# Stick-breaking attention block: a filler clock that counts all matmuls, a head norm issued in four steps, an output projection in two passes, and masks added two blocks at a time

## Chip, core and metric

The kernel runs on one core of a Trainium2 chip. The time is the device time of one execution in microseconds (us); the figure compared is the median of the timed runs. TensorE (PE) multiplies, PEld is its weight load, ScalarE (ACT) does activations, VectorE (DVE) elementwise work, GpSimd (POOL) little here, and SyncE (SP) issues the weight transfers.

## Reference, cut to what matters

The program computes two transformer blocks on 512 tokens of width 1024: block one (feed-forward, two attention branches, feed-forward), block two (feed-forward, stick-breaking attention, feed-forward). The change lies in the stick-breaking attention, 16 heads of 64 wide:

```
qkv = (xn @ w_qkv).reshape(b, s, 3, 16, 64)
q = rms_norm(qkv[:, :, 0], q_gain);  k = rms_norm(qkv[:, :, 1], k_gain);  v = qkv[:, :, 2]
z = q @ k.T / sqrt(64)                      # per head, blocks of 128 queries
mask = s_idx < t_idx                        # strictly causal
log_1m = where(mask, log_sigmoid(-z), 0)
rev_excl = reverse exclusive cumsum of log_1m over the keys
w = where(mask, exp(log_sigmoid(z) + rev_excl), 0)
o = (w @ v) over all heads;   x = x + o @ w_o
```

## The kernel before, in words

All activations are kept transposed, 128 features by 512 tokens to a tile. Every large product is done in three matmuls of 32-bit "round" type (`mm3`, lines 182 to 184): a weight chunk of 128x128 and an activation tile are each split into a high and a low part, and high x high, high x low and low x high are added in PSUM. One `mm3` on one 128-row slice is a **unit**; a tile of width 1024 needs eight. Weight chunks come in by SP in the order of the list `plan`; `split_ahead` makes the high part on ACT (line 159, "cast") and the low part on DVE (line 160), four chunks ahead of their use. PE, ACT and SP execute in the order in which the code writes them; DVE and POOL instructions are placed by the framework.

The stick-breaking stage weaves two strands. `stick()` is the attention of eight head pairs n = 0..7. `sb_dense()` is the filler: 128 units of Q and K projections (`qk_tile`), 64 units of V (`sv_tile`, six matmuls of 256 columns each), and then the first units of the output projection. `stick()` hands over at each `yield s`, whereupon `F.pull(s)` writes s filler units. `F.t` is a clock that goes on by one with each unit pulled; `F.at(d, fn)` has `fn` written when the clock has gone d further.

A head pair is written thus. `front`: 14 score matmuls (line 853), two for block 2 of the upper head (858), and eight matmuls of 128 columns that add the causal mask (862); the scores fill five PSUM banks A1, A0, Z2, B1, B0 of the eight. Then six steps t = 0..5: absolute value from PSUM (`absolute`, line 868, DVE), Exp and Ln (872, 873, ACT), `soft` (877, DVE), and the high/low split of the result (177 ACT, 178 DVE). Then `middle(…, 0)`, 20 records of cumulative-sum matmuls (887, 892, 893) on the lower head's banks, `middle(…, 1)` on the upper head's, Exp of the five banks (`weights`, 896, ACT), and `back(n-1)`, the product with V of the pair before (905), whose result is split and put in `os_` three ticks later. `front(n)` waits, in the writing, until K[n] is there; `back` until the clock is past `state["bank_free"]`.

The head norm of a Q or K tile: `first` (one tick after its eighth unit) scales the tile out of PSUM on DVE (778) and squares it on ACT (780); `second`, seven ticks later (`NORM_LAG`), sums over each head by a matmul (786, called hn below), and at once writes Ln and Exp (211, 212, ACT) and four DVE instructions (214, 215, 216, 789); nine ticks later (`SCALE_LAG`) the tile counts as there. A Q tile's K tile follows right behind it in the filler.

The output projection: `EARLY = ((0, 1), (2,))` runs tiles 0 and 1, then 2, over os_[0..6] into PSUM banks that stay taken; behind the stage tile 3 is done whole, then the last unit of 0, 1 and 2, then tiles 4 to 7. After each tile DVE adds it to x (972), and ACT and DVE prepare the next feed-forward (227 or 230, 231, 249, 250).

Of the kernel before, what the change touches and what calls it, by code (L numbers as in the profile page):

```python
# [16 lines left out]
P = 128  # L17
S = 512
D = 1024
KD = 8  # L20
# [15 lines left out]
class Flow:  # L36
# [19 lines left out]
    def pull(self, n):  # L56

        for _ in range(n):
            got = 0 if self.dense is None else next(self.dense, 0)
            self.t += 1  # L60
            self.fire()
            if got == 0:
                self.dense = None
            if got != 1:
                return False
        return True

    def settle(self):
        while self.due:
# [5 lines left out]
def block_kernel(ctx: ExitStack, tc: tile.TileContext, a, out):  # L75
# [56 lines left out]
    for kind, n in SB_ORDER:  # L132
        if kind == "v":
            sv_chunks(n)
        else:
            plan.append((a["sb_qk"][n], 1024))
            plan.append((a["sb_qk"][8 + n], 1024))
    for m in range(KD):
        plan.append((a["sb_o"][m], 1024))
    for n in range(2 * NF):  # L140
        plan.append((a["f4_in"][n], 1024))
# [627 lines left out]
    def qk_tile(n, which, g):  # L769
        ps = bank()  # L770
        yield from proj(ps, a["sb_qk"][n], 1024, zs)
        if "r2" not in state:
            state["r2"] = nx.rstd()
            F.at(7, lambda: column_of(state["r2"], rcol2))

        def first():
            t = sl()
            dve.tensor_tensor(t, ps, state["r2"], op=OP.mult)
            sq = sl()
            act.activation(sq, t, AF.Square)  # L780
            F.at(NORM_LAG, lambda: second(t, sq))

        def second(t, sq):
            pm = bank()
            state["bank_free"] = F.t + 6
            pe.matmul(pm, halves, sq, start=True, stop=True)  # L786
            rs = sl()
            rsqrt(rs, pm, 1.0 / 64)
            dve.scalar_tensor_tensor(t, t, g, rs, op0=OP.mult, op1=OP.mult)
            if which is K:  # L790
                pool.tensor_copy(kz[n % 3][HALF[1], :], t[HALF[1], 2 * P:3 * P])
            F.at(SCALE_LAG, lambda: which.__setitem__(n % 8, t))
        F.at(1, first)

    def sb_dense():
        for kind, n in SB_ORDER:
            if kind == "v":
                yield from sv_tile(n)
            else:
                yield from qk_tile(n, Q, qg)  # L800
                yield from qk_tile(8 + n, K, gains[:, 57:58])

        for ms in EARLY:
            for m in ms:
                early.append((bank(), weight(a["sb_o"][m], 1024)))
            split_ahead(SPLIT_AHEAD + 1 - len(early))
            for k in range(7):
                while os_[k] is None:
                    yield 2
                for m in ms:  # L810
                    ps, (wh, wl) = early[m]
                    c = slice(k * P, (k + 1) * P)
                    mm3(ps, wh[:, c], wl[:, c], *os_[k], k == 0, False)
                    yield 1

    early = []
    os_ = [None] * KD
    HALF = (slice(0, 64), slice(64, 128))
    kz = [consts.tile([P, P], F32, name=f"kz{i}") for i in range(3)]
# [7 lines left out]
    ident_r = consts.tile([P, P], F32R, name="ident_r")  # L827
    dve.tensor_copy(ident_r, ident)

    hidden_r = consts.tile([P, P], F32R, name="hidden_r")  # L830
    dve.scalar_tensor_tensor(hidden_r, later, NEG, ident_n, op0=OP.mult, op1=OP.add)
    nlater = consts.tile([P, P], F32, name="nlater")
    dve.scalar_tensor_tensor(nlater, later, -1.0, ident, op0=OP.mult, op1=OP.subtract)
    nones = consts.tile([P, P], F32, name="nones")
# [7 lines left out]
    def stick():  # L842

        def front(n):

            q, k = Q[n], K[n]
            z = [bank() for _ in range(5)]
            started = set()  # L850
            for g, sb in ((0, 1), (1, 1), (0, 3), (1, 3), (0, 0), (1, 0), (0, 2)):
                b, c = AT[g][sb]
                pe.matmul(z[b][:, c:c + S - sb * P], k[HALF[g], sb * P:(sb + 1) * P], q[HALF[g], sb * P:],  # L853
                          start=b not in started, stop=True, skip_group_check=True)
                started.add(b)

            b, c = AT[1][2]
            pe.matmul(z[b][:, c:c + 2 * P], kz[(8 + n) % 3], q[:, 2 * P:], start=False, stop=True, skip_group_check=True)
            for sb in (1, 3, 0, 2):
                for g in range(2):  # L860
                    b, c = AT[g][sb]
                    pe.matmul(z[b][:, c:c + P], ident_r, hidden_r, start=False, stop=True, skip_group_check=True)
            return z

        def absolute(z, b):

            t = sl()
            dve.tensor_scalar(t.bitcast(I32), z[b].bitcast(I32), 0x7FFFFFFF, None, op0=OP.bitwise_and)
            return t

        def log_part(t):
            act.activation(t, t, AF.Exp, scale=-1.0)
            act.activation(t, t, AF.Ln, bias=1.0)

        def soft(t, z):

            dve.scalar_tensor_tensor(t, z, 0.0, t, op0=OP.max, op1=OP.add)

        def middle(z, sp, hl, g):
            for j in ((3, 1, 0, 2), (3, 1, 2, 0))[g]:  # L880
                bj, cj = AT[g][j]
                w = S - j * P
                for sb in range(j, -1, -1):
                    b, c = AT[g][sb]
                    dst = z[b][:, c + (j - sb) * P:c + (j - sb) * P + w]
                    if w == P:
                        pe.matmul(dst, nlater if j == sb else nones, sp[bj][:, cj:cj + w], start=False, stop=True,
                                  skip_group_check=True)
                        continue
                    hi, lo = hl[bj]  # L890
                    m = nlater_r if j == sb else nones_r
                    pe.matmul(dst, m, hi[:, cj:cj + w], start=False, stop=True, skip_group_check=True)  # L892
                    pe.matmul(dst, m, lo[:, cj:cj + w], start=False, stop=True, skip_group_check=True)  # L893

        def weights(z, t, b):
            act.activation(t[b], z[b], AF.Exp)

        def back(n, t):

            po = bank()  # L900
            for sb in range(4):
                for g in range(2):
                    b, c = AT[g][sb]
                    cv = (sb % 2) * 256 + (n % 2) * P + g * 64
                    pe.matmul(po[HALF[g], sb * P:], v[sb // 2][n // 2][:, cv:cv + 64], t[b][:, c:c + S - sb * P],  # L905
                              start=sb == 0, stop=sb == 3)
            pair = split(po)
            F.at(3, lambda: os_.__setitem__(n, pair))

        last = None  # L910
        for n in range(KD):
            while n not in K and F.pull(1):
                pass
            while n not in K:
                F.t += 1
                F.fire()
            z = front(n)
            sp, hl = {}, {}
            order = (A1, A0, Z2, B1, B0)
            for t in range(6):  # L920

                for b in order[:2] if t == 0 else order[t + 1:t + 2]:
                    sp[b] = absolute(z, b)
                if t < 5:
                    log_part(sp[order[t]])
                if 1 <= t:
                    soft(sp[order[t - 1]], z[order[t - 1]])
                if 2 <= t < 5:
                    hl[order[t - 2]] = split(sp[order[t - 2]])
                yield 3 if t < 4 else 1  # L930
            middle(z, sp, hl, 0)
            hl[B1] = split(sp[B1])
            yield 1
            hl[B0] = split(sp[B0])
            yield 3
            weights(z, sp, A1)
            weights(z, sp, A0)
            middle(z, sp, hl, 1)
            for b in (B1, Z2, B0):
                weights(z, sp, b)  # L940
            yield 1
            if n:
                while F.t < state["bank_free"] and F.pull(1):
                    pass
                while v[1][(n - 1) // 2] is None and F.pull(1):
                    pass
                back(n - 1, last)
            yield 2
            last = sp
        yield 7  # L950
        back(KD - 1, last)
# [7 lines left out]

    norm = Norm()  # L960
    xs = [None] * KD
    ne = len(early)
    for m in [ne] + list(range(ne)) + list(range(ne + 1, KD)):
        if m < ne:
            ps, (wh, wl) = early[m]
            c = slice(7 * P, 8 * P)
            mm3(ps, wh[:, c], wl[:, c], *os_[7], False, True)
            split_ahead()
        else:
            ps = bank()  # L970
            run(proj(ps, a["sb_o"][m], 1024, os_))
        dve.tensor_tensor(x[m], ps, x[m], op=OP.add)
        norm.add(x[m])
        xs[m] = scaled_split(x[m], gain(G_F2, m))
# [16 lines left out]
ROPE_LAG = 10  # L991
STACK_LAG = 5
BACK = 3
NORM_LAG = 7
SCALE_LAG = 9
VALUE_LAG = 4
EARLY = ((0, 1), (2,))
MIX_HEAD = [T_KI, 0, 1, 2, 3]
MIX_BODY = [T_QA, T_KA, T_QA + 1, T_KA + 1, T_QA + 2, T_KA + 2, T_QA + 3, T_KA + 3, T_QB, T_QB + 1, T_QB + 2,
            T_QB + 3, T_KB] + list(range(T_GA, T_GA + 16))  # L1000
# [88 lines left out]
```

## Time and profile before

| | us |
|---|---|
| median of 3 runs (lowest, highest) | 2160.03 (2158.42, 2160.56) |
| the profiled execution | 2160.37 |
| its span in the trace | 2158.6 |
| the stick-breaking stage in it (end of feed-forward three to the last `back`) | about 1481 to 1758 |

The span runs from the first to the last instruction; what the execution takes beyond it is 1.8 us. A view by windows gives, for a stretch that one chooses, the time in which each engine had an instruction running. PE instructions overlap at their ends, so the time from one start to the next, not the duration, is what a matmul costs in a row of matmuls.

### The profile page before, as it was taken

What the parts mean: (1) busy time and instruction counts of PE and PEld (TensorE: products, weight loads), DVE (VectorE), ACT (ScalarE), POOL (GpSimd) and SP (SyncE); (2) the same over time, 40 slices, a digit from 0 to 9 for tenths busy, and PEclk for the clock granted to TensorE, in tenths of its full rate; (3) what the DMA queues carried; (4) which work ended last, traced back from release to release, by engine and by line L of the source; (5) the groups of instructions that cost most, each with busy time, mean ns of one, the idle gap of its engine ahead of it and who ended that gap; (6) DMA issues with size and microseconds to landing.
All of it is one profiled execution on the core that took longest, in us unless ns stands there. A gap on an engine that the chain in (4) does not pass through costs nothing.

```text
span 2158.6 us, 24839 instructions
## 1 busy us (share of the span) xinstructions
PE 2124.3 (98%) x10038; PEld 1748.6 (81%) x10038; DVE 1092.6 (51%) x1608; ACT 827.8 (38%) x1287; POOL 11.9 (1%) x42
## 2 busy tenths in 40 slices
PE   8999999999999999999999999999999999999999
PEld 6888888887888888888888888887777778888887
DVE  6444334699944744443445444345675556444322
ACT  5222222376766432222333222224564544222211
POOL 0000000000000000000000000000000000000000
PEclk9999999999999999999999999999999999999999
DMA  4333333322212333333333333332111113333331
GB/s 163 107 97 98 90 100 110 107 79 74 80 49 74 113 103 95 96 97 93 97 94 98 97 98 95 98 100 79 49 40 49 40 57 110 98 98 98 91 120 54
DMA packets 57266, 193.42 MB, mean 90 GB/s; under 512 B 6784, under 2 KB 6784, under 8 KB 57152
## 3 DMA queue, kind: packets, MB, share of 16 engines
q1 hardware_dynamic: 55296, 188.28, 28.1%
q0 software_dynamic: 640, 2.10, 0.3%
q8 instruction: 78, 1.28, 0.2%
q10 hardware_dynamic: 1216, 1.47, 0.2%
q14 instruction: 36, 0.29, 0.0%
HBM read 189.07 MB, written 2.10 MB: 89 GB/s over the span
## 4 chain that ended last, share of the span: by engine, by line
PE 89%; DVE 7%; ACT 3%; issue 1%; DMA 0%; ACTq 0%; DVEq 0%
PE ps L182 27%; PE ps L183 27%; PE ps L184 27%; DVE wl L160 1%; PE ps L905 1%; PE ps L853 1%; PE ps L542 1%; DVE sl L497 1%; PE ps L599 1%; PE ps L893 1%; PE ps L530 1%; DVE m L495 1%; PE ps L786 0%; PE ps L892 0%; PE ps L754 0%
## 5 line engine op out<-in xcount | busy, mean ns | idle before, releaser
L182 PE MATMUL ps<-sl,wh 128*128 128x512 f32 x2704 | 1069.7, 396 | 6.6 <-ACT sl L249 6.6
L183 PE MATMUL ps<-sl,wh 128*128 128x512 f32 x2704 | 1056.7, 391 | 1.7 <-DVE sl L250 1.6
L184 PE MATMUL ps<-sl,wl 128*128 128x512 f32 x2704 | 1056.1, 391 | 0.0
L182 PEld LDWEIGHTS ps<-sl,wh 128*128 128x128 f32 x2704 | 510.1, 189 | 116.2 <-issue 6.6
L183 PEld LDWEIGHTS ps<-sl,wh 128*128 128x128 f32 x2704 | 510.2, 189 | 107.9 <-issue 3.4
L184 PEld LDWEIGHTS ps<-sl,wl 128*128 128x128 f32 x2704 | 509.8, 189 | 107.7
L159 ACT ACTIVATE wh<-wraw 128x1024 fp32r<-128x1024 f32 (+3 forms) x368 | 372.8, 1015 | 534.0 <-issue 242.4
L160 DVE TENSOR_TENSOR wl<-wraw,wh 128x1024 fp32r<-128x1024 f32 (+3 forms) x368 | 431.4, 1174 | 283.2 <-ACT wh L159 282.6
L177 ACT ACTIVATE sl<-sl 128x512 fp32r<-128x512 f32 x145 | 90.0, 627 | 388.9 <-DVE sl L279 384.0
L279 DVE TENSOR_TENSOR sl<-ps,sl 128x512 f32<-128x512 f32 x88 | 60.8, 691 | 267.1 <-PE ps L184 260.7
L178 DVE TENSOR_TENSOR sl<-sl 128x512 fp32r<-128x512 f32 x145 | 99.0, 689 | 67.9 <-ACT sl L177 67.4
L277 DVE TENSOR_TENSOR sl<-ps,sl 128x512 f32<-128x512 f32 x88 | 60.8, 690 | 138.8 <-PE ps L184 138.7
L230 ACT ACTIVATE sl<-x 128x512 f32<-128x512 f32 x42 | 25.8, 627 | 114.0 <-DVE x L299 97.5
L298 DVE SCALAR_TENSOR_TENSOR sl<-ps,sl 128x512 f32<-128x512 f32 x32 | 22.1, 691 | 79.9 <-PE ps L184 79.9
L278 ACT ACTIVATE sl<-sl 128x512 f32<-128x512 f32 x88 | 54.1, 615 | 12.2 <-DVE sl L277 12.1
L516 ACT ACTIVATE sl<-sl,mx 128x128 f32<-128x128 f32 (+3 forms) x64 | 35.7, 558 | 41.4 <-DVE mx L515 41.2
L523 ACT ACTIVATE sl<-sl,sm 128x128 f32<-128x128 f32 (+3 forms) x64 | 35.9, 560 | 25.3 <-DVE sm L522 14.8
L599 PE MATMUL ps<-sl 128*128 128x256 f32 (+2 forms) x176 | 43.2, 327 | 0.8 <-DVE mx L515 0.8
L231 DVE TENSOR_TENSOR sl<-sl 128x512 f32<-128x512 f32 x49 | 33.3, 690 | 18.7 <-ACT sl L230 18.2
L754 PE MATMUL ps<-wh,sl 128*128 128x256 f32 x128 | 40.4, 316 | 0.0
L599 PEld LDWEIGHTS ps<-sl 128*128 128x128 f32 x176 | 33.1, 189 | 8.6 <-DVE mx L515 1.3
L214 DVE SCALAR_TENSOR_TENSOR sl<-sl 128x512 f32<-128x512 f32 x23 | 15.9, 692 | 46.9 <-ACT sl L212 46.8
(136 smaller groups left out, 1291.0 us busy)
## 6 DMA issues: line engine op xcount, KB each, us to landing
wraw<-in_f_in_dram SPq DMA_DIRECT2D x176, 512.0 KB
wraw<-in_f_out_dram SPq DMA_DIRECT2D x64, 512.0 KB
wraw<-in_mix_t_dram SPq DMA_DIRECT2D x34, 512.0 KB
wraw<-in_f_out_dram SPq DMA_DIRECT2D x32, 384.0 KB
wraw<-in_sb_qk_dram SPq DMA_DIRECT2D x16, 512.0 KB
wraw<-in_br_dram SPq DMA_DIRECT2D x16, 256.0 KB
wraw<-in_w_out_dram SPq DMA_DIRECT2D x8, 512.0 KB
wraw<-in_sb_v_dram SPq DMA_DIRECT2D x8, 512.0 KB
```

What stands on the lines that cost most here:

```text
L159: act.activation(wh[:, :n], raw[:, :n], AF.Copy)
L160: dve.tensor_tensor(wl[:, :n], raw[:, :n], wh[:, :n].bitcast(F32), op=OP.subtract)
L177: act.activation(h, x, AF.Copy)
L178: dve.tensor_tensor(l, x, h.bitcast(F32), op=OP.subtract)
L182: pe.matmul(ps, wh, xh, start=start, stop=False)
L183: pe.matmul(ps, wh, xl, start=False, stop=False)
L184: pe.matmul(ps, wl, xh, start=False, stop=stop)
L277: dve.tensor_tensor(g, pg, rs, op=OP.mult)
L278: act.activation(g, g, AF.Silu)
L279: dve.tensor_tensor(g, pu, g, op=OP.mult)
L599: pe.matmul(ps[:, :n], q[:, i * P:(i + 1) * P], part[:, :n], start=x_ == 0, stop=x_ == 1)
L754: pe.matmul(dst, hh, wh[:, cl], start=kk == 0 and b == 0, stop=False)
```

## The change

- `F.tick(n)` moves the clock on by n without pulling filler. It is called with 4 behind `front`, 4 behind the first `middle`, 2 behind the second and 3 behind `back`.
- The head norm is written in four steps: scaling on DVE; two ticks later the square on ACT; `NORM_LAG` (now 4) later the matmul; two ticks later Ln, Exp and the DVE instructions; `SCALE_LAG` (now 8) later the tile is there. `bank_free` is set to eight ticks behind the matmul instead of six.
- The masks of the blocks that lie in one bank are added by one matmul: two of 128 columns (A0, B0), and three of 256 columns (A1, Z2, B1) whose output is two separate runs of 128 columns in the bank. `hidden_r` is doubled for it by one more DVE instruction, once.
- The absolute value of A1 and B1 moves from DVE to ACT (`AF.Abs`).
- At step t = 4 two filler units are pulled where it was one, and at t = 5 likewise.
- The output projection runs in two passes. Tiles 0 to 4 take their first 5, 5, 6, 6, 6 slices while the stage runs, and DVE adds them to x; behind the stage tile 5 is done whole, then the remaining 3, 3, 2, 2, 2 slices of tiles 0 to 4, then tiles 6 and 7. The weight chunks of tiles 0 to 4 are loaded and split in two parts each.

```diff
+    def tick(self, n):
+        for _ in range(n):
+            self.t += 1
+            self.fire()
...
-    for m in range(KD):
+    for m, w in enumerate(SBO_K):
+        plan.append((a["sb_o"][m][:, :w * P], w * P))
+    plan.append((a["sb_o"][len(SBO_K)], 1024))
+    for m, w in enumerate(SBO_K):
+        plan.append((a["sb_o"][m][:, w * P:], 1024 - w * P))
+    for m in range(len(SBO_K) + 1, KD):
         plan.append((a["sb_o"][m], 1024))
...
         def first():
             t = sl()
             dve.tensor_tensor(t, ps, state["r2"], op=OP.mult)
+            F.at(2, lambda: second(t))
+
+        def second(t):
             sq = sl()
             act.activation(sq, t, AF.Square)
-            F.at(NORM_LAG, lambda: second(t, sq))
-
-        def second(t, sq):
+            F.at(NORM_LAG, lambda: third(t, sq))
+
+        def third(t, sq):
             pm = bank()
-            state["bank_free"] = F.t + 6
+            state["bank_free"] = F.t + 8
             pe.matmul(pm, halves, sq, start=True, stop=True)
+            F.at(2, lambda: fourth(t, pm))
+
+        def fourth(t, pm):
             rs = sl()
             rsqrt(rs, pm, 1.0 / 64)
...
-        for ms in EARLY:
-            for m in ms:
-                early.append((bank(), weight(a["sb_o"][m], 1024)))
-            split_ahead(SPLIT_AHEAD + 1 - len(early))
-            for k in range(7):
+        for m, w in enumerate(SBO_K):
+            ps = bank()
+            wh, wl = weight(a["sb_o"][m][:, :w * P], w * P)
+            for k in range(w):
                 while os_[k] is None:
                     yield 2
-                for m in ms:
-                    ps, (wh, wl) = early[m]
-                    c = slice(k * P, (k + 1) * P)
-                    mm3(ps, wh[:, c], wl[:, c], *os_[k], k == 0, False)
-                    yield 1
+                c = slice(k * P, (k + 1) * P)
+                mm3(ps, wh[:, c], wl[:, c], *os_[k], k == 0, k == w - 1)
+                if k == w - 1:
+                    split_ahead()
+                yield 1
+            F.at(1, lambda m=m, ps=ps: dve.tensor_tensor(x[m], ps, x[m], op=OP.add))
...
-            for sb in (1, 3, 0, 2):
-                for g in range(2):
-                    b, c = AT[g][sb]
-                    pe.matmul(z[b][:, c:c + P], ident_r, hidden_r, start=False, stop=True, skip_group_check=True)
+            for b in (A1, A0, Z2, B1, B0):
+                blocks = z[b].rearrange("p (a c) -> p a c", a=4)
+                n_ = 1 if b in (A0, B0) else 2
+                blocks = blocks[:, 0:1] if n_ == 1 else blocks[:, 0:3:2] if b == Z2 else blocks[:, 0:4:3]
+                pe.matmul(blocks, ident_r, hidden_r[:, :n_ * P].rearrange("p (a c) -> p a c", a=n_), start=False,
+                          stop=True, skip_group_check=True)
...
         def absolute(z, b):
             t = sl()
+            if b in (A1, B1):
+                act.activation(t, z[b], AF.Abs)
+                return t
...
             z = front(n)
+            F.tick(4)
...
-                yield 3 if t < 4 else 1
+                yield 3 if t < 4 else 2
             middle(z, sp, hl, 0)
+            F.tick(4)
...
             middle(z, sp, hl, 1)
+            F.tick(2)
...
                 back(n - 1, last)
+                F.tick(3)
...
-    ne = len(early)
-    for m in [ne] + list(range(ne)) + list(range(ne + 1, KD)):
-        if m < ne:
-            ps, (wh, wl) = early[m]
-            c = slice(7 * P, 8 * P)
-            mm3(ps, wh[:, c], wl[:, c], *os_[7], False, True)
-            split_ahead()
-        else:
-            ps = bank()
-            run(proj(ps, a["sb_o"][m], 1024, os_))
+    ne = len(SBO_K)
+    for m in [ne] + list(range(KD)):
+        if m == ne and xs[m] is not None:
+            continue
+        ps = bank()
+        w = SBO_K[m] if m < ne else 0
+        src = a["sb_o"][m][:, w * P:] if w else a["sb_o"][m]
+        run(proj(ps, src, 1024 - w * P, os_[w:], 0, KD - w))
...
-NORM_LAG = 7
-SCALE_LAG = 9
+NORM_LAG = 4
+SCALE_LAG = 8
-EARLY = ((0, 1), (2,))
+SBO_K = (5, 5, 6, 6, 6)
```

## Rows read from the trace of the kernel before

**Rows 1.** The page: busy time of each engine, and the chain that ended last, by engine.

```profile
PE 2124.3 (98%) x10038; PEld 1748.6 (81%) x10038; DVE 1092.6 (51%) x1608; ACT 827.8 (38%) x1287; POOL 11.9 (1%) x42
PE 89%; DVE 7%; ACT 3%; issue 1%; DMA 0%; ACTq 0%; DVEq 0%
```

**Rows 2.** Windows: stretch and length, busy us (instructions) of PE, PEld, DVE, ACT, POOL, granted clock.

```profile
1736.00:1757.80 21.80, 21.80 (x132) 16.24 (x130) 13.04 (x20) 12.65 (x22) 0.00 (x0) 1.00 0.15 49
1757.80:1800.00 42.20, 42.20 (x188) 34.92 (x187) 24.90 (x33) 19.02 (x27) 0.00 (x0) 1.00 0.30 94
```

**Rows 3.** Waits of PE, 1481 to 1758: total us, times, longest.

```profile
PE ps L892 <- ACT sl L177: 9.9, 9, 2.5
PE ps L893 <- DVE sl L178: 6.0, 12, 0.8
```

**Rows 4.** Windows of PE alone: the eight `middle` with waits, first, longest, sum.

```profile
1516.48:1521.90 5.42, 3.82 (x22) 1.00 0.00 1
...
1712.47:1720.06 7.59, 4.31 (x23) 0.79 0.10 40
sum 45.92, PE 29.97; mean PE 3.75
```

**Rows 5.** Windows of PE alone: the filler behind four of them, low clock, first and sum.

```profile
1551.62:1556.60 4.98, 4.98 (x13) 0.52 0.34 96
...
sum 15.47, PE 15.47; mean PE 3.87
```

**Rows 6.** Windows of PE alone: 48 filler matmuls, mask, `middle`, 42 V matmuls, whole `front`.

```profile
1470.11:1480.99 10.88, 10.88 (x50) 1.00 0.23 89
1505.00:1506.03 1.03, 1.03 (x11) 1.00 0.33 131
1525.60:1528.37 2.77, 2.77 (x23) 1.00 0.12 49
...
1600.93:1606.01 5.08, 5.08 (x44) 1.00 0.00 0
...
1627.72:1631.45 3.73, 3.73 (x26) 1.00 0.02 4
```

**Rows 7.** Waits of ACT, 1481 to 1758.

```profile
ACT sl L780 <- DVE sl L778: 38.7, 13, 3.6
...
ACT sl L211 <- PE ps L786: 19.1, 12, 5.9
```

**Rows 8.** Timeline at 1502: start, us, engine, line, what, [idle before].

```profile
1502.42 0.63 ACT L212 ACTIVATE sl<-sl 128x512 f32<-128x512 f32 x1
1503.09 0.69 DVE L214 SCALAR_TENSOR_TENSOR sl<-sl 128x512 f32<-128x512 f32 x1 [0.70 <-ACT sl L212]
...
1505.15 0.68 DVE L778 TENSOR_TENSOR sl<-ps,sl 128x512 f32<-128x512 f32 x1
...
1505.87 0.64 ACT L780 ACTIVATE sl<-sl 128x512 f32<-128x512 f32 x1 [2.81 <-DVE sl L778]
```

**Rows 9.** Groups of instructions, 1481 to 1758: busy us, mean ns | idle before.

```profile
L873 ACT ACTIVATE sl<-sl 128x512 f32<-128x512 f32 x40 | 25.3, 632 | 1.3
L159 ACT ACTIVATE wh<-wraw 128x1024 fp32r<-128x1024 f32 x24 | 25.1, 1045 | 0.1
L177 ACT ACTIVATE sl<-ps 128x512 fp32r<-128x512 f32 x8 | 4.8, 597 | 18.4 <-PE ps L905 18.4
```

**Rows 10.** The chain that ended last: a head-norm matmul, its two records together.

```profile
1652.88 0.86 PE ps L786 x2
```

**Rows 11.** Groups of instructions on DVE, 1757.8 to 1800.

```profile
L160 DVE TENSOR_TENSOR wl<-wraw,wh 128x1024 fp32r<-128x1024 f32 x9 | 10.9, 1220 | 5.2 <-ACT wh L159 5.2
L972 DVE TENSOR_TENSOR x<-ps,x 128x512 f32<-128x512 f32 x8 | 5.4, 685 | 10.6 <-PE ps L184 10.5
```

**Rows 12.** Table loads in the whole trace, by groups: the line that loads for Silu.

```profile
L278 ACT ACT_TABLE_LOAD x4 | 5.1, 1283 | 0.1
```

More of the change, by code (lines that the diff above doesn't have):

```diff
@@ L801, in sb_dense @@
                 yield from qk_tile(8 + n, K, gains[:, 57:58])
-        for ms in EARLY:
-            for m in ms:
-                early.append((bank(), weight(a["sb_o"][m], 1024)))
-            split_ahead(SPLIT_AHEAD + 1 - len(early))
-            for k in range(7):
+        for m, w in enumerate(SBO_K):
+            ps = bank()
+            wh, wl = weight(a["sb_o"][m][:, :w * P], w * P)
+            for k in range(w):
                 while os_[k] is None:
                     yield 2
-                for m in ms:
-                    ps, (wh, wl) = early[m]
-                    c = slice(k * P, (k + 1) * P)
-                    mm3(ps, wh[:, c], wl[:, c], *os_[k], k == 0, False)
-                    yield 1
-    early = []
+                c = slice(k * P, (k + 1) * P)
[4 more added lines that the diff above has]
+            F.at(1, lambda m=m, ps=ps: dve.tensor_tensor(x[m], ps, x[m], op=OP.add))
     os_ = [None] * KD
@@ L828, in block_kernel @@
     dve.tensor_copy(ident_r, ident)
-    hidden_r = consts.tile([P, P], F32R, name="hidden_r")
-    dve.scalar_tensor_tensor(hidden_r, later, NEG, ident_n, op0=OP.mult, op1=OP.add)
+    hidden_r = consts.tile([P, 2 * P], F32R, name="hidden_r")
+    for c in range(2):
+        dve.scalar_tensor_tensor(hidden_r[:, c * P:(c + 1) * P], later, NEG, ident_n, op0=OP.mult, op1=OP.add)
     nlater = consts.tile([P, P], F32, name="nlater")
```

## The prediction, as put on record before the changed kernel was run

> **What bounds the kernel now.** I read the page first: PE has an instruction running for 98% of the span, and 89% of the chain that ended last is PE's [rows 1]. The end can come earlier only if PE does less or stops waiting. Next I looked for stretches in which PE waits within the stick-breaking stage, since the change touches nothing else. There the view of waits has only two entries, 15.9 us together, and both are the matmuls of `middle`: they wait for the high part (ACT, line 177) and the low part (DVE, 178) of a split [rows 3]. The reader should see that nothing else waits: scores, masks, `back` and filler run without a gap.
>
> What these waits cost is more than the 15.9 us. A `middle` without a wait takes 2.77 us [rows 6]; the eight that wait take 45.92 us together, 45.92 - 8 x 2.77 = 23.8 us too much [rows 4]. Behind four of them the filler runs at a granted clock of 0.52 to 0.61, near the lower of the two levels, 1.2 instead of 2.4 GHz: PE had just stood idle inside the `middle`. These four stretches last 15.47 us [rows 5] and hold 30 matmuls of 512 and 18 of 256 columns, which at full clock cost 10.88/48 = 0.227 and 5.08/42 = 0.121 us each [rows 6], 9.0 us together; 6.5 us is lost. So the stage loses **30.2 us**, and that is all that better timing can bring.
>
> Why are the splits late? ACT works in the written order, and in the stage it stands 38.7 us because a Square (780) was written directly behind its DVE scaling (778), and 19.1 us because a Ln (211) was written directly behind its matmul (786) [rows 7]. What stands behind them, Exp, Ln and splits of the running head, is late by as much. The counter-example is the last head: no head norm is left there, and its two `middle` have no wait (that window is busy throughout, 21.80 of 21.80 us) [rows 2].
>
> **The change, part by part.**
>
> *Masks.* Eight matmuls of 128 columns take 1.03 us, 0.129 each [rows 6]. Two of these stay, and three of 256 columns come: 2 x 0.129 + 3 x 0.121 = 0.62 us, 0.41 less per head, 3.3 us over eight, all on PE's path. The bounds are 3.3 and 0: the trace has no matmul whose output is in two runs, and if such a one costs as two single blocks, nothing is gained. I take 3.3, since moving data and column count are those of the 256-column row. The Trainium skill speaks against it: PSUM — Partial Sum Buffer, section Specifications (TRN2), says that an access pattern that is not contiguous slows matmuls significantly. By the row the term is 3.3 us; by that rule it goes towards 0 and the sum ends 3.3 us higher; no row of this trace decides it.
>
> *Order of the head norm.* The Square now comes two ticks, some 1.4 us, behind its scaling, and Ln two ticks behind its matmul. Of the 38.7 us (13 waits, 3.0 each) the Square sheds about half; of the 19.1 (12 waits, 1.6 each) nearly all goes. But only four ticks are left between Square and matmul where there were seven, so PE itself may now wait for a Square. I counted the clock's steps through the new code and walked the queues in head 4, from the end of `front`. PE: eleven three-matmul units (0.68 each), five V units of six matmuls (0.73) and a head-norm matmul of 0.86 [rows 6, 10], so the second head-norm matmul could start at 12.0 us. ACT, in its order: two absolute values (0.60 each), four Exp-Ln pairs (1.25), two casts (1.05), one Square (0.63), two splits (0.62) and Ln with Exp of the Q tile (1.3): 11.5 us by durations, a little less since neighbours overlap at their ends. Durations are those of [rows 8, 9], the absolute value at that of an ACT instruction that reads PSUM (597 ns), Ln, Exp and split at that of line 873. Then DVE: the K tile's scaling is written behind the Q tile's four norm instructions and gets in after three of them, 2.8 us after the Exp [rows 8], then the Square, 0.64. That is 14 to 14.9 us, and PE waits 2 to 2.9 us, behind which the whole first `middle` queues. The splits for that `middle` are there by then, so it doesn't wait again. Walked in the same way, heads 0 and 2 wait about 2 us, 3 and 5 about 1 and 1.5, and 1, 6 and 7 not at all. I take 8.5 us, and 1.5 for one stretch of low clock behind one of them (6.5/4 each before): **10 us remain of the 30.2**. The bounds are 0 and the rival below.
>
> *Clock and filler.* The ticks write nothing by themselves. They let the tiles be there earlier in PE's time, so that filler is kept for later; the first `front` comes after 33 units as before. Between `front` and the first `middle` 16 units are pulled instead of 13 or 14, 1.4 to 2 us more cover for ACT, which is in the walk. What is pulled there is missing later: of the 28 first-pass units (21 before) the last two come between the last head's two `middle`, and nothing is left behind them. Before, not one unit lay between those two, and neither waited [rows 2].
>
> *Absolute value.* Sixteen DVE instructions become sixteen on ACT at 0.60: 1.2 us more per head in ACT's order, in the walk. DVE is relieved by as much.
>
> *Two passes.* PE's units stay 64; 52 followed the last `back` before, 36 now, the others fill the heads. DVE gets five more additions (0.685 [rows 11]), which lie beside filler; without cover they would cost 3.4 us. Weights are moved in five more transfers of the same bytes in all; SP's queue holds only weight loads here, in the order of use. The tail is dense before: all 42.20 us busy [rows 2]. Afterwards tiles 5, 0, 1, 2, 3, 4, 6, 7 take 8, 3, 3, 2, 2, 2, 8, 8 units, 24.5 us, and DVE has per tile an addition, the sum of squares and a low part (0.69, 0.69, 0.75) and a weight split of up to 1.22. From tile 0 on it falls behind, catches up in 6 and 7, and ends the last tile 29 to 30 us in; the feed-forward wants that tile as its eighth slice at 24.5 + 7 x 0.68 = 29.3. I take 1 us, bounds 0 and 4: ACT's casts wait for loads here, and a load that is late by one chunk costs some units more.
>
> *The rest:* the head-norm bank is held two ticks longer; the code pulls filler meanwhile, so PE loses nothing, or up to 1.4 us per head if that filler were missing at the end. One DVE instruction more at the start is hidden.
>
> **Sum.** 30.2 - 10 + 3.3 - 1 = 22.5 us. Against the profiled execution (2160.4; its span is 1.8 us less) that is 2137.9, and the median stands 0.3 below it: **2138 us**.
>
> **The rivals.**
>
> *The Square takes the wait over.* For it: where a K tile follows its Q tile with no `front` between, the Q tile's norm instructions still lie ahead of the K tile's scaling on DVE, and the new code has the matmul earlier. If all five heads wait 3.2 us and four get the low clock (1.6), 22 us remain; with half of the mask and 1 us of tail the gain is 30.2 - 22 + 1.6 - 1 = 9, so 2151 (2146 to 2155.7). Against it: the Ln waits go and the cover grows.
>
> *It does not do what it says.* ACT's work, not its order, makes the splits late; then more filler and new order shift the waits only, and the masks are what is left: 2156 to 2164, say 2157. Against it: ACT is busy 12.65 of 21.80 us in the head without a wait [rows 2].
>
> *Slower: the absolute value needs another function table on ACT.* A table load takes 1283 ns [rows 12]. Two absolute values per head, each between Exp and Ln, would bring four loads, 5.1 us in front of the last split. The walk of head 4 has that split at 13.4 us where PE wants it at about 14; it would wait some 4.5 us in eight heads, 36 us, with eight times 1.6 of low clock 49, against 30.2 now: 49 - 30.2 - 3.3 + 1 = 16 us slower, 2177. The gain is gone from about 2.8 us per head on. Against it: Square, copy, Exp and Ln are mixed in this stage, and the group of every ACT instruction in it has no load among it [rows 9]. The Trainium skill's page ScalarE: Activation LUTs, section Table sets: the hidden batching unit, says that cheap functions, abs among them, are in every set; by that rule this rival falls; no row shows an Abs.
>
> **How the numbers follow.** Forecast (2131 to 2146) 0.68; the Square 0.20; does nothing 0.07; slower 0.05. Faster than 0.2%, 4.3 us, which is about what a measurement of this kernel can tell: the first two, 0.88. The lower end is everything recovered with a little of the unknown, 30.2 + 3.3 = 33.5, 2127, rounded up by the tail to 2128; the upper end takes in most of the Square's range, 2152.
>
> **What would show it.** Right: the waits of 177 and 178 at `middle` nearly gone, ACT waiting for 778 half as long and for 786 hardly, five mask matmuls in 0.62 us, a new entry in PE's waits, the head-norm matmul for the Square, of under 10 us. Wrong: that entry at 15 us or more; table loads in the stage; PE waiting for DVE at the start of the last feed-forward; a mask group that still takes 1 us.

## The result, and the profile after

The changed kernel took 2133.95 us (median; 2133.72 to 2135.77), the kernel before 2160.18 on the same chip: a ratio of 0.9883 (95% interval 0.9871 to 0.9895), 26.2 us less. Forecast were 2138 and a range of 2128 to 2152. The span fell from 2158.6 to 2131.8 us, 26.8.

A window over the whole stage shows where. First the kernel before, then the changed one (stretch and length, busy us and instructions of PE, PEld, DVE, ACT, POOL, the granted clock, DMA share, GB/s):

```profile
1481.00:1757.80 276.80, 260.85 (x1460) 205.33 (x1458) 170.26 (x254) 147.85 (x241) 2.33 (x8) 0.96 0.15 48
```

```profile
1481.00:1741.10 260.10, 255.90 (x1483) 205.10 (x1481) 164.65 (x247) 156.46 (x261) 3.00 (x8) 1.00 0.16 49
1741.10:1777.30 36.20, 35.77 (x158) 29.29 (x157) 25.39 (x34) 20.18 (x28) 0.00 (x0) 1.00 0.43 133
```

PE had nothing running for 15.95 us of the stage before (276.80 - 260.85) and for 4.2 us after, and the granted clock is 1.00 throughout. The stage is 16.7 us shorter and holds 16 more units of the output projection (36 follow the last `back` instead of 52), 16 x 0.68 = 10.9 us. That is 27.6 us together against 26.8 of the span; a wait of 0.4 us in the tail takes back half of the difference. The waits of PE answer to [rows 3] (who waited for whom, us in all, times, longest):

```profile
PE ps L801 <- ACT sl L795: 2.9, 2, 1.6
PE ps L916 <- DVE sl L189: 1.3, 3, 0.6
PE ps L194 <- DVE sl L261: 0.4, 1, 0.4
```

Lines 915 and 916 of the changed kernel are 892 and 893 of the one before, 801 the head-norm matmul, 795 its Square. The wait for a high part is gone, that for a low part has fallen from 6.0 to 1.3 us; the Square is new. Windows of PE alone: the three `middle` that still wait, and the last one, in the terms of [rows 4]:

```profile
1618.18:1621.62 3.44, 3.05 (x22) 1.00 0.00 0
1642.62:1646.28 3.66, 3.04 (x22) 1.00 0.28 107
1650.01:1653.33 3.32, 3.04 (x22) 1.00 0.00 0
1733.75:1736.62 2.87, 2.87 (x21) 1.00 0.00 0
```

Against 2.77 us each they lose 2.1 and 0.1 us, where eight lost 23.8. No stretch behind them runs at the low clock ([rows 5] had 6.5 us there). The two waits for a Square, and the mask group:

```profile
1520.80:1524.21 3.41, 2.16 (x16) 1.00 0.51 154
1576.42:1584.22 7.80, 6.15 (x45) 1.00 0.26 71
1504.55:1505.26 0.71, 0.71 (x7) 1.00 0.00 0
```

The first holds twelve V matmuls (1.45 us at 0.121) and 0.56 of the head-norm matmul's 0.86 us, the second 42 (5.08) and the whole 0.86: they lose 1.4 and 1.9 us. The masks take 0.71 us where [rows 6] had 1.03. ACT's waits answer to [rows 7]; 790 is the scaling, 222 the Ln, 889 the absolute value that waits for the masks:

```profile
ACT sl L795 <- DVE sl L790: 27.5, 12, 3.0
ACT sl L889 <- PE ps L881: 21.0, 6, 4.4
...
ACT sl L222 <- PE ps L801: 15.6, 11, 4.9
```

The Square's wait has fallen by 11 us only, the Ln's by 3.5. ACT stood for 58 us behind lines 778 and 786 before and stands for 43 behind 790 and 801 now, although the middles have lost nearly all of their waits.

The sum closes: of the 30.2 us lost before, 2.2 + 3.3 + 0.4 = 5.9 are still lost; 30.2 - 5.9 = 24.3, and the masks give 8 x 0.32 = 2.6. Together 26.9, against 26.8 of the span.

### The profile page after: what moved, and what is told of

It reads as the page before. It is cut to its first block, busy times and chain, and to the rows that moved or that the text cites. A ratio compares the mean times of both kernels' runs of the same rounds, so it can differ in the third digit from the quotient of the medians.

```text
span 2131.8 us, 24835 instructions
## 1 busy us (share of the span) xinstructions
PE 2107.0 (99%) x10014; PEld 1737.6 (82%) x10014; DVE 1086.9 (51%) x1603; ACT 836.6 (39%) x1308; POOL 12.6 (1%) x42
## 4 chain that ended last, share of the span: by engine, by line
PE 89%; DVE 7%; ACT 2%; issue 1%; DMA 1%; ACTq 0%; DVEq 0%
PE ps L193 27%; PE ps L194 27%; PE ps L195 27%; DVE wl L171 1%; PE ps L928 1%; DVE sl L508 1%; PE ps L871 1%; PE ps L916 1%; PE ps L553 1%; DVE m L506 1%; PE ps L915 1%; PE ps L610 1%; PE ps L765 1%; PE ps L801 1%; PE ps L766 1%
## 5 line engine op out<-in xcount | busy, mean ns | idle before, releaser
L170 ACT ACTIVATE wh<-wraw 128x1024 fp32r<-128x1024 f32 (+4 forms) x373 | 373.9, 1004 | 519.4 <-issue 234.4
L171 DVE TENSOR_TENSOR wl<-wraw,wh 128x1024 fp32r<-128x1024 f32 (+4 forms) x373 | 432.4, 1161 | 284.0 <-ACT wh L170 280.8
L225 DVE SCALAR_TENSOR_TENSOR sl<-sl 128x512 f32<-128x512 f32 x23 | 15.9, 692 | 51.8 <-ACT sl L223 51.8
L610 PEld LDWEIGHTS ps<-sl 128*128 128x128 f32 x176 | 32.9, 188 | 8.5 <-DVE mx L526 1.2
```

Source lines behind the costliest of these rows:

```text
L170: act.activation(wh[:, :n], raw[:, :n], AF.Copy)
L171: dve.tensor_tensor(wl[:, :n], raw[:, :n], wh[:, :n].bitcast(F32), op=OP.subtract)
L610: pe.matmul(ps[:, :n], q[:, i * P:(i + 1) * P], part[:, :n], start=x_ == 0, stop=x_ == 1)
```

## The experiments

Each run undoes or adds one part, so that its share shows. All are compared with runs of the kernel before on the same chip; the changed kernel's ratio is 0.9883. Line numbers shift a little from kernel to kernel.

**One part alone, in the kernel before.** The masks:

```diff
-            for sb in (1, 3, 0, 2):      # eight matmuls of 128 columns
+            for b in (A1, A0, Z2, B1, B0):   # five, as in the change
```

> The kernel before with the two-block masks alone. In the changed kernel a mask group took 0.71 us instead of 1.03, so the theory that PE is the bound in every head expects 8 x 0.32 = 2.6 us less than before (about 2157.6), with the waits of the first middle unchanged. The rival, that a head's length is set by ACT's chain which starts when the masks end, expects the same 2.6 us, since the masks lie ahead of that chain; a time that does not move (within 1 us of before) would refute both and leave the masks without effect.

2157.65 us, ratio 0.9989 (0.9981 to 0.9998), 2.1 us less by medians, 2.4 by the ratio. The middles wait as before (16.1 us in all). The interval holds the expected 2.6 us and not zero; this run doesn't tell the two theories apart, as was said.

The head norm in four steps:

```diff
+            F.at(2, lambda: second(t))        # Square two ticks behind its scaling
...
+            F.at(2, lambda: fourth(t, pm))    # Ln, Exp two ticks behind the matmul
-NORM_LAG = 7
-SCALE_LAG = 9
+NORM_LAG = 4
+SCALE_LAG = 8
```

> The kernel before with the head norm in four steps (lags 4 and 8) alone: no ticks, no extra filler, masks, absolute values and output projection as before. If ACT's written order was the cause of the late splits, this alone takes back a good half of the 30 us: 2140 to 2148, and ACT's waits of line 780 and 211 fall from 58 us to under 40. The rival, that cover (more units between front and the first middle, ticks, filler kept for the last heads) is what helped, expects less than 5 us of gain: 2155 or more.

2148.53 us, 0.9948 (0.9936 to 0.9961): 11.2 us less, half a microsecond outside what the order was to bring and far from the rival; ACT's waits of 780 and 211 fall from 58 to 42 us, where under 40 was expected. Its waits of PE:

```profile
PE ps L893 <- DVE sl L883: 5.4, 4, 1.5
PE ps L899 <- DVE sl L178: 3.6, 8, 0.8
PE ps L898 <- ACT sl L177: 1.7, 3, 1.1
PE ps L789 <- ACT sl L783: 0.6, 1, 0.6
```

The old waits for splits are down from 15.9 to 5.3 us, and a new one stands first: line 893 is the very first matmul of a `middle`, and it waits for `soft` (883). Windows show which: the two `middle` of heads 6 and 7, with nothing between them.

```profile
1713.06:1722.63 9.57, 7.82 (x40) 6.62 (x41) 6.27 (x10) 7.79 (x16) 0.00 (x0) 0.82 0.00 1
1731.44:1741.02 9.58, 6.93 (x40) 5.36 (x40) 6.27 (x10) 7.79 (x16) 0.00 (x0) 1.00 0.01 2
```

Two middles take 5.54 us without a wait; these take 9.6 each. Only two filler units lay between `front` and them: the filler had run out. It was used earlier, ahead of `back`: in head 3 PE works for 22.3 us (1625.83 to 1648.16) between the second `middle` and `back`, where the changed kernel has 0.79. This edit also sets `bank_free` two ticks later and has no ticks to pass them, so the 11.2 us hold both what the order brings and what the lost filler costs.

The ticks:

```diff
             z = front(n)
+            F.tick(4)
...
+            F.tick(4)    # behind middle 0; 2 behind middle 1, 3 behind back
```

> The kernel before with the ticks alone: lags 7 and 9, Square and Ln written directly behind what they wait for, one unit at steps 4 and 5, projection and masks as before. If the ticks work by keeping filler (the back that waits for its bank no longer pulls many units, so that filler lasts for the heads) but need the written order of ACT and the cover as well, they bring little alone: 0 to 6 us less than before, 2153 to 2160. The rival, that the clock by itself is the gain (the changed kernel without it was 13 us slower), expects 10 us or more: under 2150.

2159.51 us, 0.9999 (0.9990 to 1.0008): nothing. The splits wait as ever, and with the lags of before the matmul comes early enough for one wait on the Square:

```profile
PE ps L898 <- ACT sl L183: 7.3, 6, 2.5
PE ps L899 <- DVE sl L184: 6.6, 13, 1.1
PE ps L792 <- ACT sl L786: 2.0, 1, 2.0
```

**One part undone, in the changed kernel.** The ticks:

```diff
     def tick(self, n):
-        for _ in range(n):
-            self.t += 1
-            self.fire()
+        pass
```

> The changed kernel with the ticks writing nothing and moving nothing (the clock counts filler units only). If the order of ACT is the cause, the ticks matter little: 0 to 5 us slower than the changed kernel, 2134 to 2139. The rival, that the clock which counts all matmuls is what lets the norm be done in time and filler be kept, expects at least 10 us more: 2144 or more, with waits back at the middles.

2147.30 us, 0.9940 (0.9927 to 0.9954): 12 to 13 us of the gain go, so my low price for the ticks was wrong and the rival right. Most of them go where the filler has run out: the middles of heads 5 to 7 lose 9.7 us, where they lose 0.1 in the changed kernel. The rest goes in heads 0 to 2, where PE waits 4.9 us for a Square instead of 2.9 and the first `middle` of head 1 takes 2.2 us longer. Without ticks the clock passes `bank_free` only by pulling units, so many are used ahead of a `back` (in head 3, 21.0 us of PE's work from 1630.60 to 1651.57, instead of 0.79); in head 5 only nine filler matmuls lie between `front` and the first middle, and its two middles take 12.27 us instead of 5.54, at a granted clock of 0.72:

```profile
1697.14:1709.41 12.27, 9.57 (x41) 7.57 (x41) 6.27 (x10) 8.62 (x17) 0.00 (x0) 0.72 0.00 1
```

The Square and Ln written directly behind what they wait for, with the same total lag:

```diff
-            F.at(2, lambda: second(t))
-        def second(t):
             sq = sl()
             act.activation(sq, t, AF.Square)
-            F.at(NORM_LAG, lambda: third(t, sq))
+            F.at(NORM_LAG + 2, lambda: third(t, sq))
...
-            F.at(2, lambda: fourth(t, pm))
-        def fourth(t, pm):
```

> The changed kernel with the Square again written directly behind its scaling and Ln directly behind its matmul, at the same total lag (6 ticks to the matmul, 10 to the end). If ACT's order is the cause, 10 to 18 us of the gain go: 2144 to 2152, and ACT waits for the scaling 35 us or more again. The rival (cover and clock) expects under 4 us of loss: 2134 to 2138.

2143.98 us, 0.9926 (0.9913 to 0.9938): 9 to 10 us go, at the lower edge of what ACT's order led me to expect, and more than twice what cover and clock alone allow. ACT waits for the scaling 32.9 us, a little under the 35 expected, and PE for the Square twice as long:

```profile
PE ps L798 <- ACT sl L792: 6.0, 5, 2.4
PE ps L909 <- ACT sl L188: 1.9, 2, 1.4
PE ps L910 <- DVE sl L189: 1.9, 5, 0.4
```

The filler units at steps 4 and 5:

```diff
-                yield 3 if t < 4 else 2
+                yield 3 if t < 4 else 1
```

> The changed kernel with one filler unit instead of two at steps 4 and 5, thus 14 units of cover instead of 16 between front and the first middle. If cover is what keeps the middles free of waits, ACT is late by up to 1.4 us in the heads that have no slack: 2 to 8 us more, 2136 to 2142. The rival, that ACT's order alone removed the waits, expects no more than 1 us.

2142.14 us, 0.9925 (0.9913 to 0.9938): 8 to 9 us go. The waits for both parts of the splits are back, worst in head 6 (its first middle 5.82 us instead of 2.77):

```profile
PE ps L916 <- DVE sl L189: 3.5, 7, 1.1
PE ps L801 <- ACT sl L795: 3.4, 2, 2.4
PE ps L915 <- ACT sl L188: 2.8, 2, 2.1
```

So the order of ACT doesn't remove the waits without cover; the rival of that run falls.

The output projection of before:

```diff
-SBO_K = (5, 5, 6, 6, 6)
+EARLY = ((0, 1), (2,))    # with its plan, its first pass and its end as before
```

> The changed kernel with the output projection of before (tiles 0 and 1, then 2, over seven slices, last slices behind the stage): 21 first-pass units instead of 28. The run without ticks lost 12 us where filler ran out in the last heads, so the theory that filler must last expects the last heads to run uncovered here too: 3 to 10 us more than the changed kernel, 2137 to 2144, the loss at the middles of heads 6 and 7. The rival, that the two passes only move units from behind the stage into it, expects no more than 1 us of difference.

2141.29 us, 0.9917 (0.9904 to 0.9931): 7 us go; the loss was expected in heads 6 and 7, and all that the trace shows of it lies in head 7. There two units of filler are left between `front` and the middles, which take 10.41 us in one stretch (1722.37 to 1732.78) instead of 5.54, and PE waits 0.9 us more for the split behind `back`. The timeline of PE there (start, us, engine, line, what, idle before):

```profile
1722.37 0.49 PE L906 MATMUL ps<-sl,nlater 128*128 128x128 f32 x2 [0.88 <-DVE sl L896]
1725.21 1.01 PE L906 MATMUL ps<-sl,nones 128*128 128x128 f32 x3 [2.35 <-DVE sl L896]
```

The absolute value on DVE again:

```diff
-            if b in (A1, B1):
-                act.activation(t, z[b], AF.Abs)
-                return t
```

> The changed kernel with the absolute values of A1 and B1 on DVE again. The walk of the queues puts 1.2 us per head on ACT for them and takes as much from DVE; ACT's lag behind PE decides, so my theory expects 0 to 4 us less time (2130 to 2134), above all at the head-norm matmuls that wait for a Square. The rival, that DVE is the queue which is late (the Square waits for a scaling on DVE behind the norm's instructions), expects 2 to 8 us more: 2136 to 2142.

2134.57 us, 0.9885 (0.9872 to 0.9899): no difference that can be measured. Neither theory's larger numbers came; moving 1.2 us per head between ACT and DVE is worth nothing here.

The masks in the changed kernel:

```diff
-            for b in (A1, A0, Z2, B1, B0):
+            for sb in (1, 3, 0, 2):      # eight matmuls of 128 columns, as before
```

> The changed kernel with the eight masks of 128 columns each again. The masks alone brought about 2 us in the kernel before, and their group took 0.32 us less. If PE is the bound in the heads of the changed kernel, all of it is lost: 8 x 0.32 = 2.6 us more than the changed kernel, 2136 to 2138. The rival, that ACT's chain, which starts when the masks of A1 end, takes back what PE saves, expects less than 1 us of difference: 2134 to 2135.

2137.12 us, 0.9893 (0.9880 to 0.9907), 2 to 3 us more; the span is 3.5 us longer. The intervals overlap, so the times alone don't settle it, but every mask group takes 1.03 us again and the sum, 2.6, fits.

**The disputed cost of the masks.**

```diff
-                blocks = blocks[:, 0:1] if n_ == 1 else blocks[:, 0:3:2] if b == Z2 else blocks[:, 0:4:3]
+                blocks = blocks[:, 0:n_]
```

> The changed kernel with the three two-block masks written to 256 adjoining columns of the bank instead of two separate runs, so that the masks of the second blocks fall on wrong columns (the output is not the reference's): it measures what an output in two runs costs. The forecast priced such a matmul at 0.121 us, as 256 adjoining columns; the group then took 0.71 us instead of 0.62. If the two runs cost the missing 0.09 us (three times 0.03), the group takes 0.62 us here. The rival, that the two-run output is free and the group's excess lies elsewhere (in the change from and to other shapes), expects 0.71 us again.

This kernel puts the masks of the second blocks on wrong columns; it ran once, for the durations (2133.53 us). The timeline of PE; the group lasts from its start to that of the next matmul:

```profile
1504.50 0.88 PE L881 MATMUL ps<-hidden_r,ident_r 128*128 128x256 f32 x5
1505.21 0.45 PE L193 MATMUL ps<-sl,wh 128*128 128x512 f32 x1
```

0.71 us, as with two runs: here the output in two runs is free, and the 0.09 us above the forecast lie elsewhere. The starts of the single matmuls show where. In all eight groups of this kernel and of the changed one the first takes 0.30 to 0.31 us to the next start, the others 0.06, 0.17, 0.12 and 0.06. In the kernel before the first of the eight takes 0.25 and the others 0.11 each. So the first matmul of a group costs more than its successors; the forecast's 0.129 had spread that over eight, and its 0.121 came from a row of 42 equal ones. Why the first one is dear no run separates.

**Further on.** The two waits for a Square show a concrete cause, in the rows of head 0 (all three engines, in order of start):

```profile
1520.91 0.69 DVE L226 SCALAR_TENSOR_TENSOR sl<-ps,sl 128x512 f32<-128x512 f32 x1
1521.64 0.69 DVE L227 SCALAR_TENSOR_TENSOR sl<-sl 128x512 f32<-128x512 f32 x1
1522.25 0.68 DVE L790 TENSOR_TENSOR sl<-ps,sl 128x512 f32<-128x512 f32 x1
```

```profile
1522.96 0.63 ACT L795 ACTIVATE sl<-sl 128x512 f32<-128x512 f32 x1 [2.81 <-DVE sl L790]
```

```profile
1523.65 1.13 PE L801 MATMUL ps<-sl,cmat 128*128 128x512 f32 x2 [1.25 <-ACT sl L795]
```

The K tile's scaling (790) sits behind the Q tile's norm instructions (226, 227), since both are written at the same tick, the norm first. One tick more between Square and matmul undoes the tie:

```diff
-NORM_LAG = 4
-SCALE_LAG = 8
+NORM_LAG = 5
+SCALE_LAG = 7
```

> The changed kernel with the Square one tick further ahead of its matmul (NORM_LAG 5, SCALE_LAG 7, the sum as before). The K tile's scaling is then written ahead of the Q tile's norm instructions on DVE, and the matmul has five ticks instead of four, so PE's two waits for a Square (2.9 us) should go: 2130 to 2132. The rival, that the wait only moves to the tile's end (a front that waits for its K tile) or to the middles, expects no gain: 2134 or more.

2131.67 us, 0.9871 (0.9856 to 0.9886): 2 to 3 us less than the changed kernel by medians (the intervals overlap), and the wait is gone from the trace, as the theory has it: ACT waits 12.8 us for the scaling instead of 27.5, PE no longer for the Square. The middles of heads 3 and 4 no longer wait either; those of head 2 do instead and lose 2.5 us. This is the fastest version of those run, with the next one beside it. What is left:

```profile
PE ps L916 <- DVE sl L189: 1.8, 3, 0.8
PE ps L194 <- DVE sl L261: 0.6, 1, 0.6
```

To the same kernel, one more absolute value on ACT:

```diff
-            if b in (A1, B1):
+            if b in (A1, Z2, B1):
```

> The kernel with NORM_LAG 5 and SCALE_LAG 7, and Z2's absolute value on ACT too. What waits are left there (1.8 us, at the two middles of head 2) end with the low part of a split on DVE; if DVE's queue is what is late there, taking one more instruction per head off it brings 0 to 2 us: 2129.5 to 2131.5. The rival, that ACT is then late in its place, expects 1 to 4 us more: 2133 to 2136.

2131.89 us, 0.9869 (0.9856 to 0.9883): the same. The waits at the middles of head 2 stay (2.2 us), still on the low part from DVE, so one instruction less on DVE does not cure them. What does is open.

## Why the prediction was right, point by point

**What can be won.** The account of 30.2 us, waits and low clock together, held: what is still lost and what was won add up to it within 0.1 us. The low clock, put at one stretch of 1.5 us, didn't appear (granted clock 1.00 over the stage).

**The Square takes the wait over.** The new entry came where the walk put it for heads 0 and 2: 1.4 and 1.9 us against "about 2 us". For heads 3, 4 and 5 it was mis-sized at 4.5 us, and the cause is a step of the walk: that the second head-norm matmul of head 4 stands ahead of the first `middle`, "behind which the whole first `middle` queues". It is written behind it. The four ticks behind the middle are what bring it due, so the middle goes first and covers the wait for the Square; in heads 3 and 5 too it follows right behind the first `middle` (1614.56 and 1675.34). Head 4:

```profile
1645.58 0.39 PE L916 MATMUL ps<-sl,nlater_r 128*128 128x256 f32 x1 [0.62 <-DVE sl L189]
...
1646.28 1.02 PE L801 MATMUL ps<-sl,cmat 128*128 128x512 f32 x2
```

Here the matmul (801) follows its middle without a wait. In return the middles of heads 3 and 4 still wait 2.1 us for low parts, which the walk had as done. Together 5.5 us were left in the heads instead of 10; with 0.6 less lost in the tail and 0.7 less won by the masks these 4.5 us account for the 4 us by which the forecast was too high.

**Order of the head norm.** The Square was to shed half of its 38.7 us and the Ln nearly all of its 19.1. They shed 11.2 and 3.5, so two of the signs named for "right" did not come. The middles lost their waits all the same; that ACT now waits where PE has filler is my reading of it, and no run shows it by itself. That ACT's order was a cause is shown (11 us alone, 9 to 10 undone); that it was the cause is not: undoing the cover or the ticks costs about as much. Cover alone, the two passes alone and pairs of parts were not run.

**Clock and filler.** "The ticks write nothing by themselves" is true and led me to price them at nothing beyond the walk, although the same paragraph says that they keep filler for later. The kernel needs them: without them 12 to 13 us go, though alone they bring nothing. What they do is to keep filler, as the stretches ahead of `back` show. The step that failed is the one on `bank_free`, where I let the code pull filler at no cost "or up to 1.4 us per head if that filler were missing at the end": it would have been missing.

**Masks.** 2.6 us instead of 3.3: a group takes 0.71 us, not 0.62, because the prices of 0.129 and 0.121 are means of longer rows and leave out most of what a group's first matmul costs. The run with adjoining columns shows that the two-run output isn't the reason. So what the Trainium skill says in PSUM — Partial Sum Buffer, Specifications (TRN2), that a pattern which isn't contiguous slows matmuls significantly, is not borne out for an output in two runs of 128 columns (0.71 us with them and without); the measurement decides.

**Absolute value.** No table load stands in the stage, so the slower rival fell; and moving the two instructions has no effect on the time that can be measured. The Trainium skill says in ScalarE: Activation LUTs, Table sets: the hidden batching unit, that abs is in every set; the trace agrees (16 instructions of 577 to 598 ns, none with a load before it).

**Two passes and the tail.** PE waits 0.4 us for the low part of the last tile, in the feed-forward's first product, as walked (1 us was taken). That the passes are worth 7 us in the last head, by the filler that they leave for it, was not in the sum as a term.

The parts don't add: the four that matter cost 7 to 13 us each when undone, some 38 us together, more than the whole gain. All four of these runs lose more at the middles than the changed kernel does, so the parts protect the same places.

That the sum came out within 4 us is in part luck. It starts from all that PE loses and takes off new waits only, so it doesn't ask which part does the work: the ticks, the units at steps 4 and 5 and the two passes stand in it with no term of their own, and each turned out to be needed.

## What to carry to other kernels

In a woven kernel the filler is a stock: ask of every edit how many units it uses before the last place that needs cover, not only whether it hides something where it stands. An instruction on an in-order queue is best written when what it waits for is surely done; but look whom its lateness reaches next, and whether a tie of two due times puts it behind a longer chain. Parts that protect the same place should be tried by undoing them one by one in the final version as well as alone, since alone they may show nothing.

## What the hardware did that I had not expected

A matmul of 256 columns whose output goes to two separate runs of 128 columns takes as long as one with adjoining output: both groups 0.71 us. The first matmul of such a group costs 0.30 us to the next start, where the later ones cost 0.06 to 0.17. And PE's idle times of 1.25 and 1.65 us, one in each of two heads, left the granted clock at 1.00, where before a middle with several waits was followed by 0.52 to 0.61 in four cases of eight; what makes the difference no run here separates. The length of one wait doesn't settle it: in the run without ticks a wait of 2.15 us for a Square was followed by 3.35 us at a granted clock of 0.50 (1574.96 to 1578.31), in the run with one unit at steps 4 and 5 a wait of 2.35 us by a clock of 1.00 (1578.09 to 1583.22).
